# The opening of a hybrid decoder kernel, reordered: three row tiles in the first norm batch, a constant that loads ScalarE's table, parameters and decays behind the first products

## The chip, the cores and the metric

The kernel runs on one core of a Trainium2 chip. A core has engines that run side by side, each working off its own queue in order: TensorE (PE in the profile; its weight loads are PEld), VectorE (DVE), ScalarE (ACT), GpSimd (POOL), and SyncE (SP), which here issues nearly all DMAs. Products land in PSUM; VectorE and ScalarE can read it, and GpSimd's operands here lie in SBUF. The metric is the time of one execution on the device in microseconds.

## The reference, cut to what matters

One inference step of a decoder with one recurrent (RG-LRU) layer and one attention layer, for a prompt of 2048 tokens and 64 new tokens of 8 running sequences. Everything is f32 with a model width of 1024. Only the recurrent layer's beginning is touched:

```python
def rms_norm(x, g):
    xf = x.astype(jnp.float32)
    y = xf * lax.rsqrt(jnp.mean(xf * xf, axis=-1, keepdims=True) + EPS)
    return (y * g.astype(jnp.float32)).astype(x.dtype)

def recurrent_mixer(x, h0, conv_buf, w_in, conv_w, conv_b, w_ga, b_ga, w_gx, b_gx, lam, w_out):
    z = x @ w_in                                  # x is rms_norm(x, a_pre_norm)
    u, g = z[..., :D_RNN], z[..., D_RNN:]
    u, new_buf = causal_conv(u, conv_buf, conv_w, conv_b)
    h, h_last = rg_lru(u, h0, w_ga, b_ga, w_gx, b_gx, lam)
    return (h * jax.nn.silu(g)) @ w_out, h_last, new_buf
...
# in rg_lru, r and i are sigmoids of block products of u:
    log_a = -RGLRU_C * r * jax.nn.softplus(-lam.astype(jnp.float32))
    a = jnp.exp(log_a)
    inp = jnp.sqrt(-jnp.expm1(2.0 * log_a)) * (i * uf)
    # h is the running scan h <- a * h + inp
```

After the recurrent layer come the shared keys and values, attention of the prompt over itself, attention of the new tokens over a paged cache of 4096 rows per sequence, and the output projection.

## The kernel before, in words

The prompt is worked off in two halves of 1024 tokens. The first half takes the 64 new tokens along, so it has 1088 columns in three groups of 320, 384 and 384 columns. Its nine row tiles are the sample tile (64 rows) and eight prompt tiles of 128 rows; group 0 consists of the sample tile and two prompt tiles, groups 1 and 2 of three prompt tiles each.

`Norm0` (from L513) loads row tiles, four buffers deep (`A0_BUFS`), and normalises them in batches. ScalarE squares each tile's two halves with an accumulator (L544), VectorE adds the two sums, `rsqrt` (L222) computes the inverse root of the whole batch's column of sums by two starting operations and three Newton steps (L225 to L235), and VectorE scales each tile by the root and by the broadcast norm weight `apreB` (L552). `turned` then has TensorE transpose each tile by 128x128 blocks into PSUM (L508). ScalarE casts each block to the rounded type float32r (`xh`, L98), and VectorE writes the remainder (`xl`, L105). When a tile has been turned, its buffer's next load is issued. The first batch is made by the caller (`a00.norm(2)`), every later one by `turned`, two tiles each, so the batches hold 2, 2, 2, 2 and 1 tiles.

A product in f32 is made of three float32r products (`mm3`: high times high, high times remainder, remainder times high). Weights are split the same way: ScalarE casts a staged half of a weight (`wh`), and the remainder `wl` is written by VectorE and GpSimd in turns (`Weights.split`, L98 and L105).

`phase_a1` (L567) goes over the eight blocks of 128 recurrent channels, and in each over the three groups. For block n and a group it makes the product `u` (24 matmuls), copies it out, runs the short convolution on VectorE (`front`, L576 and L578, which reads the parameters `gv`), the gates of the group before (`gated`), the product `g`, and then the decay of the group before (`decayed`: two exponential-like activations on ScalarE that read `nsp4` and `psp4`, L614 and L615). A group's products start once `turned` has covered its columns.

`prologue` (L260) loads ten small parameters as 43 rows (L264 to L273), transposes them on TensorE in eight blocks (L276) into `gv`, and derives two halved biases. It is called through `ready` from `recur`, behind the fetch of the first weights and ahead of all products. `decays` (L282) turns the 8x128 lambdas into softplus values: one exponential on ScalarE and 25 operations on VectorE of 128x8 elements, the logarithm being a series (`log1p_into`, L240). It is traced in the first block right behind the front of group 0.

The order of the work on each engine is not written out by hand. The program is traced in the order of the code; a planner then times it with a model, and places what is ready by priority, which is the order of tracing, unless a `high_priority` block raises it. `issue_after(ins)` makes the instructions of its block on the engine of `ins` stand behind `ins`. What is placed is fixed: on the chip each engine goes through its queue in that order and waits where an operand is late.

Behind the opening follow `phase_a2` (the output product of the layer), the key, value and query projections together with the attention over the cache (`Side`, whose interleaving is set by estimated costs), the second half of the prompt, and the attention of the prompt.

Of the kernel before, what the change touches and what calls it, by code (L numbers as in the profile page):

```python
# [20 lines left out]
P = 128  # L21
D = 1024
# [5 lines left out]
H = 16  # L28
# [56 lines left out]
def tile_hawk_fox(  # L85
# [173 lines left out]

    def prologue():  # L260

        with tc.tile_pool(name="pro", bufs=1, side="right") as pro:
            rows = pro.tile([43, D], F32, name="rows")
            S.dma_start(rows[0:1, :], a_pre_norm)  # L264
            S.dma_start(rows[1:5, :], a_conv_w[0])
            S.dma_start(rows[5:6, :], a_conv_b)
            S.dma_start(rows[6:7, :], a_b_ga)
            S.dma_start(rows[7:8, :], a_b_gx)
            S.dma_start(rows[8:9, :], a_lambda)
            S.dma_start(rows[9:10, :], kv_norm.rearrange("(o d) -> o d", o=1))  # L270
            S.dma_start(rows[10:11, :], b_pre_norm)
            S.dma_start(rows[11:35, :], state_conv[0].rearrange("b j d -> (b j) d"))
            S.dma_start(rows[35:43, :], state_rnn[0])  # L273
            tp = mmp()
            for k in range(KB):
                T.transpose(tp[:, k * 43:(k + 1) * 43], rows[:, k * P:(k + 1) * P], ident[:43, :43])  # L276
# [3 lines left out]
            S.dma_start(bfB[:, :], b_f.rearrange("(o h) -> o h", o=1).broadcast_to([P, H]))  # L280

# [83 lines left out]
    def mm3(ps, lh, ll, rh, rl, nk):  # L365
        for k in range(nk):
            T.matmul(ps, lh(k), rh(k), start=(k == 0), stop=False)  # L367
            T.matmul(ps, lh(k), rl(k), start=False, stop=False)  # L368
            T.matmul(ps, ll(k), rh(k), start=False, stop=(k == nk - 1))  # L369
# [16 lines left out]
    class Weights:  # L386
# [125 lines left out]
    class Norm0:  # L512


        def __init__(self, s, pool):
            self.s, self.pool = s, pool
            self.apreB = pool.tile([P, D], F32, name="apreB")
            self.xts, self.n = [], 0
            self.load(0)
            S.dma_start(self.apreB[:, :], a_pre_norm.broadcast_to([P, D]))  # L520
            for i in range(1, A0_BUFS):
                self.load(i)
# [8 lines left out]
        def norm(self, n):  # L531
# [16 lines left out]
            tt(V, ss[:, :w], parts[:, 0, :w], parts[:, 1, :w], ALU.add)  # L548
            r = rsqrt(ss[:, :w], P, 1.0 / D, w=w)
            for k, i in enumerate(todo):  # L550
# [15 lines left out]

    def phase_a1(s, xs, a0, covered, feed, wk, out, then, begin):  # L567
        mh = s.mh
        sm = s.samp

        def front(n, c0, C, ups, us, up, W):
# [92 lines left out]
        for n in range(KB):  # L664
# [8 lines left out]
            for gi, (c0, C) in enumerate(s.groups):  # L673
# [1001 lines left out]

    def recur(s, a0, xs, covered, ex, out, then, begin, ready=None):

        with ExitStack() as ek:
            wk = sbuf(ek, f"a1_{s.i}")
            xs.extend(alloc_groups(sbuf(ex, f"xa_{s.i}"), s, len(xs), len(s.groups)))  # L1680
            feed = Feed([(a_in[n],) for n in range(KB)])
            feed.fetch()
            feed.fetch()
            if ready:
                ready()

            def turnover():
                ex.close()
                then()

            phase_a1(s, xs, a0, covered, feed, wk, out, turnover, begin)

# [26 lines left out]
    xs = []  # L1719
    recur(sca[0], a00.turned(xs, todo), xs, 0, ExitStack(), out, turn0, lambda: next(a2[0]), prologue)  # L1720
    x0.extend(alloc_x(sbuf(xe0, "xb0"), scb[0].cols))
# [119 lines left out]
```

## Time and profile before

| quantity | value |
|---|---|
| median of three runs | 3070.52 us (3066.45 to 3083.66) |
| the profiled execution | 3073.57 us |
| its span, first to last instruction | 3071.8 us |
| TensorE busy | 2826.8 us, 92% of the span |
| VectorE, ScalarE, GpSimd busy | 1805.2, 1294.9, 1158.7 us |
| mean granted TensorE clock | 0.965 |

A row of the timeline reads: start, duration, engine, line, operation, what it writes and reads, count; in brackets the idle time ahead of it and what ended that. Rows for short operations that follow each other on one engine can be merged, and their durations overlap. A row of groups has the busy time, the mean in ns, and the idle time ahead. A row of waits has the total, the number and the longest. A row of stages has the length, the busy time and count of PE, PEld, DVE, ACT and POOL, the granted clock, the share of the DMA engines' time and GB/s.

### The profile page before, as it was taken

How to read it: one execution, taken by the hardware profiler on the slowest of the kernel's cores; microseconds unless marked ns; L12 is line 12 of the kernel's file. 1: busy time of each engine (PE TensorE's matmuls, PEld its weight loads, DVE VectorE, ACT ScalarE, POOL GpSimd, SP SyncE). 2: the span in 40 equal slices, each digit the busy share in tenths (PEclk: the TensorE clock that was granted, in tenths of full speed). 3: DMA queues.
4: the chain of work that ended last, by engine and by line, in shares of the span. 5: the costliest groups of instructions: out<-in, count | busy, mean ns of one | idle time of the engine just before them, and what ended most of it. 6: DMA issues, size and time to landing. Idle time of an engine off the chain costs nothing.

```text
span 3071.8 us, 58144 instructions
## 1 busy us (share of the span) xinstructions
PE 2826.8 (92%) x20462; PEld 2178.9 (71%) x20462; DVE 1805.2 (59%) x4012; ACT 1294.9 (42%) x2874; POOL 1158.7 (38%) x1263
## 2 busy tenths in 40 slices
PE   5998999999999989997999798998989989999898
PEld 5997889988999978896888454555545554554587
DVE  7876555424357756755555566666667765543244
ACT  4665432222346655333333244343434445455321
POOL 1653201000025532000000365656565757788522
PEclk9999999999999999998999799999999999999999
DMA  4224547788622256999999998989999997322243
GB/s 121 91 76 147 157 137 209 239 256 260 209 82 86 86 180 202 318 312 313 329 311 316 303 285 258 293 276 306 294 309 316 328 286 236 107 67 68 83 143 111
DMA packets 492855, 653.25 MB, mean 213 GB/s; under 512 B 91100, under 2 KB 292829, under 8 KB 485286
## 3 DMA queue, kind: packets, MB, share of 16 engines
q1 hardware_dynamic: 488934, 643.87, 66.8%
q10 hardware_dynamic: 3340, 3.56, 0.4%
q8 instruction: 162, 2.65, 0.4%
q0 software_dynamic: 288, 2.10, 0.2%
q14 instruction: 131, 1.07, 0.1%
HBM read 513.82 MB, written 135.16 MB: 211 GB/s over the span
## 4 chain that ended last, share of the span: by engine, by line
PE 56%; DMA 18%; DVE 10%; ACT 6%; SPq 5%; issue 4%; POOL 2%; DVEq 0%; ACTq 0%; POOLq 0%
PE ops L1558 6%; DMA raw<-in_cache_k_dram 4%; PE y L367 4%; PE y L368 4%; PE y L369 4%; PE st L1538 4%; DMA raw<-in_cache_v_dram 4%; PE sx L1405 3%; PE kv L369 3%; PE kv L367 3%; PE kv L368 3%; PE dO L1236 3%; PE st L1539 3%; PE dS L1126 2%; PE qg L367 2%
## 5 line engine op out<-in xcount | busy, mean ns | idle before, releaser
L105 POOL TENSOR_TENSOR acc<-acc,p 128x512 f32<-128x512 f32 (+3 forms) x576 | 640.6, 1112 | 304.6 <-PE ops L1558 240.8
L1547 ACT ACTIVATE p<-st 128x512 f32<-128x512 f32 (+3 forms) x576 | 290.5, 525 | 409.5 <-PE st L1539 186.6
L1158 DVE STREAM_TRANSPOSE ktr<-raw 128x1024 f32<-128x1024 f32 x256 | 305.3, 1224 | 151.2 <-DMA raw<-in_cache_k_dram 141.8
L1407 DVE TENSOR_REDUCE mxs<-sx 128x1 f32<-128x512 f32 x384 | 253.6, 679 | 145.0 <-PE sx L1405 144.2
L368 PE MATMUL kv<-wl,xh 128*128 128x256 f32 (+3 forms) x1088 | 309.9, 288 | 9.0 <-DVE wl L412 8.8
L367 PE MATMUL kv<-wh,xh 128*128 128x256 f32 (+3 forms) x1088 | 311.0, 290 | 5.8 <-ACT wh L411 5.7
L369 PE MATMUL kv<-wh,xl 128*128 128x256 f32 (+3 forms) x1088 | 310.1, 287 | 0.0
L1558 PE MATMUL ops<-p,vvt 128*64 128x512 f32 (+3 forms) x1152 | 296.9, 554 | 2.3 <-ACT p L1547 2.1
L1538 PE MATMUL st<-qa,ka 128*128 128x512 f32 (+3 forms) x640 | 273.6, 428 | 21.1 <-ACT p L1547 16.6
L1405 PE MATMUL sx<-kbt,qbt 96*128 96x512 f32 (+3 forms) x640 | 232.3, 421 | 26.3 <-DMA qbt<-qd 10.6
L1538 PEld LDWEIGHTS st<-qa,ka 128*128 128x128 f32 x640 | 124.1, 194 | 179.5 <-issue 112.9
L411 ACT ACTIVATE wh<-wst,gv 128x256 fp32r<-128x256 f32 (+1 forms) x384 | 164.4, 499 | 187.7 <-DMA wst<-in_b_w_in_dram 73.2
L1539 PE MATMUL st<-qbt,kbt 128*128 128x512 f32 (+3 forms) x640 | 236.5, 371 | 0.0
L412 DVE SCALAR_TENSOR_TENSOR wl<-wst,gv,wh 128x256 fp32r<-128x256 f32 (+1 forms) x384 | 170.4, 494 | 104.6 <-ACT wh L411 100.8
L367 PE MATMUL qg<-xh,wh 128*128 128x384 f32 (+2 forms) x640 | 228.8, 359 | 0.0
L369 PE MATMUL qg<-xh,wl 128*128 128x384 f32 (+2 forms) x640 | 227.6, 357 | 1.1 <-DVE wl L412 1.0
L368 PE MATMUL qg<-xl,wh 128*128 128x512 f32 (+2 forms) x640 | 227.0, 356 | 0.0
L1091 POOL TENSOR_TENSOR qw<-qb,amask 128x128 f32<-128x128 f32 x64 | 29.8, 473 | 502.7 <-PE dS L1126 354.0
L368 PEld LDWEIGHTS kv<-wl,xh 128*128 128x128 f32 (+1 forms) x1088 | 204.3, 189 | 12.7 <-DVE wl L412 10.4
L367 PEld LDWEIGHTS kv<-wh,xh 128*128 128x128 f32 (+1 forms) x1088 | 204.3, 189 | 12.2 <-ACT wh L411 6.5
L369 PEld LDWEIGHTS kv<-wh,xl 128*128 128x128 f32 (+1 forms) x1088 | 206.0, 190 | 4.4 <-issue 4.3
L1405 PEld LDWEIGHTS sx<-kbt,qbt 96*128 96x128 f32 x640 | 117.6, 201 | 93.7 <-issue 31.1
(299 smaller groups left out, 6477.2 us busy)
## 6 DMA issues: line engine op xcount, KB each, us to landing
raw<-in_cache_k_dram SPq DMA_DIRECT2D x512, 256.0 KB
raw<-in_cache_v_dram SPq DMA_DIRECT2D x512, 256.0 KB
wst<-in_w_kv_dram SPq DMA_DIRECT2D x48, 512.0 KB
wst<-in_b_w_in_dram SPq DMA_DIRECT2D x48, 512.0 KB
xt<-in_x_prompt_dram SPq DMA_DIRECT2D x32, 512.0 KB
wst<-in_a_w_in_dram SPq DMA_DIRECT2D x64, 256.0 KB
out_dram<-kf SPq DMA_DIRECT2D x128, 128.0 KB
sc<-cd SPq DMA_DIRECT2D x16, 1024.0 KB
```

The costliest lines, as they stand in the source:

```text
L105: eng.tensor_tensor(out, a, b, op=op)
L367: T.matmul(ps, lh(k), rh(k), start=(k == 0), stop=False)
L368: T.matmul(ps, lh(k), rl(k), start=False, stop=False)
L369: T.matmul(ps, ll(k), rh(k), start=False, stop=(k == nk - 1))
L412: V.scalar_tensor_tensor(wl[:, k, :], st[:, k, :], gk, f(wh[:, k, :]), op0=ALU.mult, op1=ALU.subtract)
L1158: V.transpose(t.kts[pp][:, n], raw[:, :, pp * 256:(pp + 1) * 256])
L1405: T.matmul(ps[:, :w], qb[0:96, j * P:(j + 1) * P], kb[0:96, ck * 512:ck * 512 + w], start=True, stop=True)
L1407: V.reduce_max(mx[:, j, ck:ck + 1], ps[:, :w], axis=AX.X)
L1538: T.matmul(ps[:, lo:], ka[:, ks], qa[:, lo:], start=True, stop=False)
L1539: T.matmul(ps[:, lo:], kb[:, ks], qb[:, lo:], start=False, stop=(k < qc * 4))
L1547: pair.append((k, lo, p, A.activation(p[:, lo:], ps[:, lo:], AF.Exp)))
L1558: return T.matmul(ops[r:r + HD, lo:], vvs[h % 2][:, k, :], p[:, lo:], start=(k < 2), stop=(last and k >= todo[-1][0] - 1))
```

## The change

Five things are done, all in the opening of the first half:

- The first batch of `Norm0` has three tiles and so all of group 0; the nine tiles go in batches of 3, 2, 2 and 2. The load of `apreB` is issued behind three tile loads and not behind one.
- The inverse root in `Norm0.norm` is placed at high priority.
- ScalarE squares one column of a constant before anything else, so that its function table is loaded then.
- `prologue` is split. `parameters` issues the DMAs at the place where `prologue` issued them (and `bfB`'s with them, as before). The transposes and what hangs on them are traced behind the first `u` product. The pool that holds the rows stays open until then.
- `decays` is traced in group 1 behind the product `g`, ahead of the decay of group 0, and its VectorE operations stand behind the first operation of group 1's front.

```diff
-    def prologue():
-        with tc.tile_pool(name="pro", bufs=1, side="right") as pro:
-            rows = pro.tile([43, D], F32, name="rows")
-            S.dma_start(rows[0:1, :], a_pre_norm)
...
+    opening = ExitStack()
+
+    def parameters():
+        rows = opening.enter_context(tc.tile_pool(name="pro", bufs=1, side="right")).tile([43, D], F32, name="rows")
+        for lo, src in ((0, a_pre_norm), (1, a_conv_w[0]), (5, a_conv_b), (6, a_b_ga), (7, a_b_gx), (8, a_lambda),
...
+            S.dma_start(rows[lo:lo + src.shape[0], :], src)
+        S.dma_start(bfB[:, :], b_f.rearrange("(o h) -> o h", o=1).broadcast_to([P, H]))
+        return rows
+
+    def prologue(rows):
+        with opening:
             tp = mmp()
             for k in range(KB):
                 T.transpose(tp[:, k * 43:(k + 1) * 43], rows[:, k * P:(k + 1) * P], ident[:43, :43])
...
-            self.load(0)
-            S.dma_start(self.apreB[:, :], a_pre_norm.broadcast_to([P, D]))
-            for i in range(1, A0_BUFS):
+            for i in range(A0_BUFS):
+                if i == 3:
+                    S.dma_start(self.apreB[:, :], a_pre_norm.broadcast_to([P, D]))
                 self.load(i)
...
-            r = rsqrt(ss[:, :w], P, 1.0 / D, w=w)
+            with tc.high_priority():
+                r = rsqrt(ss[:, :w], P, 1.0 / D, w=w)
...
-            V.tensor_scalar(uc[:, so:C], up[:, 3:3 + tn], gv[:, n, 4:5], gv[:, n, 5:6], op0=ALU.mult, op1=ALU.add)
+            begun[0] = V.tensor_scalar(uc[:, so:C], up[:, 3:3 + tn], gv[:, n, 4:5], gv[:, n, 5:6],
+                                       op0=ALU.mult, op1=ALU.add).ins
...
                 mm3(ups[:, :C], W.h(0, P), W.l(0, P), rh, rl, KB)
+                if rows is not None:
+                    prologue(rows)
+                    rows = None
...
                 uc, uh, ul = front(n, c0, C, ups, us, up, W)
-                if so and n == 0:
-                    decays()
                 if pend:
                     trti = gated()
                 gps = mmp("g")
                 mm3(gps[:, :C], W.h(P, 2 * P), W.l(P, 2 * P), rh, rl, KB)
+                if pend and sm and n == 0 and gi == 1:
+                    with tc.issue_after(begun[0]):
+                        decays()
                 if pend:
                     decayed(*trti)
...
+    A.activation(small.tile([P, 1], F32, name="first", tag="first")[:, :], ones[:, 0:1], AF.Square)
     a00 = Norm0(sca[0], sbuf(es0, "a0_0", "right"))
-    todo = a00.norm(2)
+    todo = a00.norm(3)
```

More of the change, by code (lines that the diff above doesn't have):

```diff
@@ L258, in tile_hawk_fox @@
     psum["mm"] = banks(lin, "mm0", 6)
-    def prologue():
-        with tc.tile_pool(name="pro", bufs=1, side="right") as pro:
-            rows = pro.tile([43, D], F32, name="rows")
-            S.dma_start(rows[0:1, :], a_pre_norm)
[L265 to L273, printed above, removed]
+    opening = ExitStack()
+    def parameters():
+        rows = opening.enter_context(tc.tile_pool(name="pro", bufs=1, side="right")).tile([43, D], F32, name="rows")
+        for lo, src in ((0, a_pre_norm), (1, a_conv_w[0]), (5, a_conv_b), (6, a_b_ga), (7, a_b_gx), (8, a_lambda),
+                        (9, kv_norm.rearrange("(o d) -> o d", o=1)), (10, b_pre_norm),
+                        (11, state_conv[0].rearrange("b j d -> (b j) d")), (35, state_rnn[0])):
+            S.dma_start(rows[lo:lo + src.shape[0], :], src)
[3 more added lines that the diff above has]
+        with opening:
             tp = mmp()
@@ L279, in prologue @@
             V.tensor_scalar(hb_gx[:, :], gv[:, :, 7], 0.5, 0.0, op0=ALU.mult, op1=ALU.add)
-            S.dma_start(bfB[:, :], b_f.rearrange("(o h) -> o h", o=1).broadcast_to([P, H]))
     def decays():
@@ L565, in turned, with phase_a1 @@
                 yield done
-    def phase_a1(s, xs, a0, covered, feed, wk, out, then, begin):
+    def phase_a1(s, xs, a0, covered, feed, wk, out, then, begin, rows):
         mh = s.mh
         sm = s.samp
+        begun = [None]
         def front(n, c0, C, ups, us, up, W):
@@ L1674, in tile_hawk_fox, with recur @@
     b_in[0][0].append((256, w_kv[:, 2 * D:]))
-    def recur(s, a0, xs, covered, ex, out, then, begin, ready=None):
+    def recur(s, a0, xs, covered, ex, out, then, begin):
         with ExitStack() as ek:
@@ L1683, in recur @@
             feed.fetch()
-            if ready:
-                ready()
+            rows = parameters() if s.i == 0 else None
             def turnover():
@@ L1689, in turnover @@
                 then()
-            phase_a1(s, xs, a0, covered, feed, wk, out, turnover, begin)
+            phase_a1(s, xs, a0, covered, feed, wk, out, turnover, begin, rows)
     def shared(parts, nk, early=False):
@@ L1719, in tile_hawk_fox @@
     xs = []
-    recur(sca[0], a00.turned(xs, todo), xs, 0, ExitStack(), out, turn0, lambda: next(a2[0]), prologue)
+    recur(sca[0], a00.turned(xs, todo), xs, 0, ExitStack(), out, turn0, lambda: next(a2[0]))
     x0.extend(alloc_x(sbuf(xe0, "xb0"), scb[0].cols))
```

## The prediction

> **What bounds the kernel now.** I read the page first: the span, the busy shares and the chain of waits over the whole run.
>
> ```profile
> span 3071.8 us, 58144 instructions
> PE 2826.8 (92%) x20462; PEld 2178.9 (71%) x20462; DVE 1805.2 (59%) x4012; ACT 1294.9 (42%) x2874; POOL 1158.7 (38%) x1263
> PE 56%; DMA 18%; DVE 10%; ACT 6%; SPq 5%; issue 4%; POOL 2%; DVEq 0%; ACTq 0%; POOLq 0%
> ```
>
> TensorE is busy 92% of 3071.8 us, so in most stages nothing but its work sets the end. The change touches only the start, and a share over the whole run says nothing about that. So I went to the busy time by stage, with one stage ending where TensorE stops waiting.
>
> ```profile
> 10.00:62.00 52.00, 30.32 (x183) 26.88 (x184) 47.46 (x146) 27.49 (x62) 10.95 (x16) 1.00 0.46 131
> 62.00:90.00 28.00, 28.00 (x171) 28.00 (x170) 17.31 (x36) 16.36 (x27) 11.77 (x17) 1.00 0.16 44
> 90.00:260.00 170.00, 162.73 (x974) 160.82 (x973) 136.21 (x261) 106.22 (x182) 99.55 (x144) 1.00 0.25 81
> ```
>
> The columns after the length are busy time on PE, PEld, DVE, ACT, POOL, then clock, DMA share, GB/s. From 10 to 62 us VectorE is busy 47.46 of 52 us and TensorE only 30.32. From 62 to 90 TensorE is full, and to 260 it has 162.73 of 170. The opening is VectorE's stage; what follows is TensorE's, and it starts whenever the opening lets it. The chain of waits from 5 to 62 us and the waits of TensorE say what the opening hangs on.
>
> ```profile
> by line: DVE xt L552 15.8%; DVE xl L105 11.2%; SPq L399 10.7%; DMA wst<-in_a_w_in_dram 9.2%; DMA xt<-in_x_prompt_dram 7.7%; DVE uc L578 5.2%; DVE lp_s L105 4.0%; ACT junk L544 3.8%; ACT xh L98 3.8%; PE tps L508 3.3%; issue 2.5%; DVE sp_l L1
> ```
>
> ```profile
> PE tps L508 <- DVE xt L552: 23.7, 2, 15.2
> PE tps L508 <- DVE xl L105: 4.5, 5, 2.0
> ```
>
> The scaling of the x tiles (L552) leads the chain, and TensorE waits 23.7 us for it in two waits. The timeline shows the second of them: the tile that group 0 still lacks.
>
> ```profile
> 1.86 0.58 SPq L520 DMA_DIRECT2D apreB<-in_a_pre_norm_dram  x1
> 5.16 1.28 ACT L544 ACT_TABLE_LOAD   x1 [5.16 <-DMA xt<-in_x_sample_dram]
> 8.74 0.63 ACT L544 ACTIVATE junk<-xt 128x512 bf16<-128x512 f32 x1 [0.81 <-DMA xt<-in_x_prompt_dram]
> 10.32 0.16 DVE L105 TENSOR_TENSOR ss<-sq 128x2 f32<-128x2 f32 x1 [7.94 <-ACT junk L544]
> 13.26 0.16 DVE L105 TENSOR_TENSOR ss<-sq 128x2 f32<-128x2 f32 x1 [0.40 <-ACT junk L544]
> 13.78 2.47 DVE L552 SCALAR_TENSOR_TENSOR xt<-xt,nr_y,apreB 64x1024 f32<-64x1024 f32 x2
> 16.11 2.42 POOL L105 TENSOR_TENSOR wl<-wst,wh 128x1024 fp32r<-128x1024 f32 x1 [14.29 <-ACT wh L98]
> 16.24 3.37 DVE L105 TENSOR_TENSOR wl<-wst,wh 128x1024 fp32r<-128x1024 f32 x1
> 19.64 1.05 PE L276 MATMUL mm<-ident,rows 43*128 43x43 f32 x8 [3.35 <-DMA gst<-in_a_w_ga_dram]
> 19.95 1.21 DVE L105 TENSOR_TENSOR wl<-wst,wh 128x1024 fp32r<-128x1024 f32 x1
> 26.42 2.34 POOL L105 TENSOR_TENSOR wl<-wst,wh 128x1024 fp32r<-128x1024 f32 x1 [4.00 <-ACT wh L98]
> 26.44 2.34 DVE L105 TENSOR_TENSOR lp_s<-lp_s,sp_e 128x8 f32<-128x8 f32 x1
> 29.33 2.91 DVE L552 SCALAR_TENSOR_TENSOR xt<-xt,nr_y,apreB 128x1024 f32<-128x1024 f32 x2
> 31.19 1.94 PE L508 MATMUL tps<-ident,xt 128*128 128x128 f32 x8 [8.53 <-DVE xt L552]
> 34.57 0.39 PE L368 MATMUL u<-xl,wh 128*128 128x320 f32 x1
> 41.87 1.04 PE L508 MATMUL tps<-ident,xt 128*128 128x128 f32 x8
> 61.90 0.42 PE L367 MATMUL u<-xh,wh 128*128 128x384 f32 x1
> ```
>
> Group 0 (320 columns) needs the sample tile and two prompt tiles. The second batch's sums are ready at 13.26, but its tiles are scaled at 29.33: its short operations stand in turns with splits, evictions and the decays. Group 0's products run from 34.57; group 2's begin at 61.90, the last wait of this kind.
>
> **The change part by part.** Everything is counted in VectorE's stretch up to group 2's first product, since that is where the stage that TensorE fills begins.
>
> ```profile
> L105 DVE TENSOR_TENSOR xl<-tps,xh 128x512 fp32r<-128x512 f32 x15 | 10.3, 687 | 2.7 <-ACT xh L98 2.4
> L552 DVE SCALAR_TENSOR_TENSOR xt<-xt,nr_y,apreB 128x1024 f32<-128x1024 f32 x8 | 10.4, 1333 | 0.1
> L105 DVE TENSOR_TENSOR xl<-tps,xh 128x256 fp32r<-128x256 f32 x2 | 0.8, 406 | 0.0
> L251 DVE TENSOR_SCALAR sp_l<-sp_l 128x8 f32<-128x8 f32 x6 | 1.0, 168 | 0.0
> L229 DVE SCALAR_TENSOR_TENSOR nr_t<-nr_y,nr_m 128x1 f32<-128x1 f32 x3 | 0.7, 219 | 0.1
> L233 DVE TENSOR_SCALAR nr_t<-nr_t 128x1 f32<-128x1 f32 x3 | 0.5, 152 | 0.1
> ```
>
> Four rows of the timeline, for a lone chain and for the spacing of products:
>
> ```profile
> 51.28 0.15 DVE L233 TENSOR_SCALAR nr_t<-nr_t 128x1 f32<-128x1 f32 x1
> 52.73 0.16 DVE L105 TENSOR_TENSOR nr_y<-nr_y,nr_t 128x1 f32<-128x1 f32 x1
> ...
> 62.48 0.31 PE L368 MATMUL u<-xl,wh 128*128 128x320 f32 x1
> 62.63 0.31 PE L369 MATMUL u<-xh,wl 128*128 128x320 f32 x1
> ```
>
> (1) *Three tiles in the first batch.* Nine tiles go in 3+2+2+2, four batches, not five. A batch of one tile is 12 short operations; with three of 0.219 us and nine of about 0.152 it is 2.0 us. Minus 2.0; bounds 0 (it ran in VectorE's gaps) and minus 2.5: a lone chain goes seven steps from 51.28 to 52.73, 0.207 us each, 12 of them.
>
> (2) *Start of the first batch.* The apreB transfer (512 KB) goes behind two more tiles in SP's queue, the constant takes the table load off the path. The load itself (1.28 us) buys little: ScalarE then waits 0.81 us for a tile. What buys is the transfer: 512 KB is 1.4 us at the 369 GB/s of 5 to 10 us (row below), so the first prompt tile comes at about 7.3 us, the second is squared by 10.3, and the sum is as early as before with a tile more. Scaling starts then after 15 lone operations of 0.207, at 13.5, against 13.78: minus 0.3, bounds plus 1.0 and minus 1.3. apreB, now behind 2.8 us of other transfers, is wanted at 13.5 only.
>
> ```profile
> 5.00:10.00 5.00, 0.00 (x0) 0.00 (x0) 0.00 (x0) 3.96 (x8) 0.00 (x0) 1.00 1.00 369
> ```
>
> (3) *High priority for the root.* No work goes; but group 0 is complete early: three scalings of 1.28 to 17.3, W's split 1.21 to 3.37, two evictions of 0.406 and four of 0.687 (3.6 us): products from about 23.3, not 34.57. That is 11.3 us on TensorE's first product. It is not the gain: group 1 and 2 still need VectorE's other work.
>
> (4) *Parameters behind the first products.* The eleven DMAs keep their place in SP's queue, between the weights and the gate weights: nothing for the queue. The eight transposes (1.05 us, after 3.35 us of idle) leave the place where a scaled tile stood behind them. They now stand behind 24 products and ahead of group 0's front, which waits for them and the copy, some 1.5 us; the 24 products of g (0.15 us apart, 3.5 us) cover that on TensorE, the next batch on VectorE. If the cover is gone, plus 1.5. I take 0.
>
> (5) *Decays behind group 1's front.* 25 operations of about 0.168 us are 4.2 us of VectorE; none is removed. They ran ahead of group 0's front. They now run between group 1's front and ScalarE's first exponential for group 0. ScalarE takes its queue in order, so a late result holds that exponential, the copies behind it (the last tiles' evictions among them) and TensorE. As filler between the last tiles half may fall into gaps: minus 2.1; bounds plus 5.2 (25 in a lone chain, all waited for) and minus 4.2.
>
> (6) *Gaps and collisions.* VectorE's waits for ScalarE's evictions (2.4 us) shrink as tiles come in order and their loads are issued earlier: minus 1.5, bounds 0 and minus 2.4. The 8-column lp_s operation took 2.34 us, beginning and ending with POOL's split: 2.2 us lost. With the decays moved it can't meet that split; another may. I take half, minus 1.1; bounds 0 and minus 2.2. A rule speaks against this: the Trainium skill, "SBUF — State Buffer", in its part on the shared port pair, says that a VectorE operation with two SBUF inputs and a GpSimd operation reading SBUF exclude each other, and that the loser waits for the whole of the other. The pairs at 16.11/16.24 and 26.42/26.44 agree with it. By it any root or scaling operation meets the split in lp_s's place: this term is then 0 and the sum 5.9 instead of 7.0.
>
> Sum: 2.0 + 0.3 + 2.1 + 1.5 + 1.1 = 7.0 us off the opening, and the time behind it moves with it, as TensorE is full from there. One more row bears on the restart: eight transposes took 1.94 us after 8.53 us of idle and 1.04 us at 41.87. I price a colder start of one group at 0.9 us, inside the bounds. The Trainium skill, "TensorE: Matmul & The Clock Gate", Part 1, says that an idle window of 3.4 us halves the clock until as much busy time has passed; by that an extra gap between groups 0 and 1 would cost 1.7 us and the sum would be 5.3. The clock column reads 1.00 throughout; only the durations agree.
>
> The profiled execution took 3073.57 us: its span, and 1.8 us around it. It stands 3.05 us above the median 3070.52. Its own time would be 3066.6; against the median the forecast is 3063.5 us.
>
> **The rivals.**
>
> *All of the first product's advance is carried* (0.17): VectorE's order leaves fronts behind the tiles. 11.3 us off, 3059.2; with the 4.5 us of waits on evictions too, 15.8 us, 3054.7. Against it: VectorE's 47.46 busy us of 52, of which little goes.
>
> *Nothing arrives* (0.20): group 0 early, but group 2 at 61.90 as before, because VectorE has the same tiles, splits and decays to do: 3070.5; with decays waited for in full, 5.2 more, 3075.7. For it: the chain's line.
>
> *Slower* (0.09). The order of all queues is made by a planner that times the whole program, so a shifted opening can place later work otherwise. The place is the stage where DMA is full:
>
> ```profile
> 1350.00:1425.00 75.00, 75.00 (x659) 62.54 (x648) 41.74 (x75) 26.38 (x67) 1.75 (x5) 1.00 0.98 324
> 1425.00:1500.00 75.00, 58.83 (x472) 47.62 (x471) 39.86 (x93) 21.16 (x55) 0.00 (x0) 0.84 1.03 311
> 1650.00:1725.00 75.00, 58.73 (x423) 44.22 (x421) 42.13 (x95) 17.88 (x49) 16.06 (x25) 0.86 0.99 288
> ```
>
> TensorE has 75 us in one stretch and 58.8 in two others: one stall in such a stretch is 16.2 us. One more, with no gain, makes 3086.7; it decides from about 22 us, if the opening does give its 7.
>
> *Faster by the same road* (0.12): one stall fewer, 16.2 and 7.0 off: 3047.3.
>
> **How the numbers follow.** My forecast has 0.42, the rivals 0.17, 0.20, 0.09 and 0.12. The bound of 0.5% is 15.4 us, about what a measurement of this kernel can tell from no change (the three runs shown span 17). Faster: the 0.12, and 0.04 of the first rival at its far end: 0.16. Slower: 0.09. Same: 0.75. The range leaves out the slower rival and about half of the lucky one: from 3048, just above 3047.3, to 3076, the second rival with the decays in full. The forecast's own range is 3059 to 3068.
>
> **What would show it.** After: one table load ahead of the first x tile; 15 root operations in a row at about 10.3; three scalings one after another from 13.5; group 0's products from 23.3; the parameters' transposes behind 24 products; VectorE still over 85% busy until group 2, whose first product comes at about 55 and not 62. Then the stretch to 260 looks as before, 7 us earlier. Group 2 at 50 means the first rival; at 62 or later the second, and the culprit would be seen as ScalarE waiting for nsp ahead of an xh cast. The prediction is wrong if the opening moves by 7 and the end by something else: then stages after 260 us differ.

## The result and the profile after

The changed kernel takes 3099.28 us (median of 8 runs, 3096.83 to 3114.79); the kernel before, on the same chip, 3073.61 us (8 runs, 3066.45 to 3083.66). The ratio is 1.0091 with an interval of 1.0072 to 1.011: slower, outside the range given. The profiled execution of after took 3099.08 us with a span of 3097.4; that of before had a span of 3071.8, so the traces differ by 25.6 us.

The page of the kernel after, its span, its busy times and its chain of work:

```profile
span 3097.4 us, 58151 instructions
PE 2845.5 (92%) x20462; PEld 2189.8 (71%) x20462; DVE 1808.1 (58%) x4000; ACT 1293.8 (42%) x2875; POOL 1156.2 (37%) x1263
PE 49%; DMA 17%; DVE 6%; SPq 4%; ACT 4%; issue 3%; POOL 1%; ACTq 0%; DVEq 0%; POOLq 0%
```

TensorE issues the same 20462 products, and they take 18.7 us longer (2826.8 before). So by these records most of the loss is not idle time: the same work ran slower.

Where it went is read from landmarks: the start of the same product (the n-th of its kind) in both traces. Negative is earlier than in the kernel before, in us; the number in brackets is its time there.

```
                             after
first u product      (33.0)   -2.8
group 1, first u     (46.2)   +3.5
group 2, first u     (61.9)   +3.3
first y             (278.7)   +4.3
last qg            (1695.0)   -3.1
st, 241st          (2194.1)   -0.0
st, 361st          (2419.9)  +15.6
st, 481st          (2645.1)  +29.1
last y             (3061.5)  +25.6
```

Two losses, then. The opening gives 4.3 us away instead of gaining 7; some 7 us come back between 279 and 1695. (Of all the traces shown here, that of the kernel before takes longest over this stretch: the others take 2.0 to 13.6 us less, e2 below, with the same order there, among them. So part of this is the one execution, and its cause stays open.) And 26 to 32 us are lost far away, in the attention that runs beside the decode part, in code that the diff does not touch.

**The opening.** Busy time by stage in the kernel after (columns as in the prediction), and the two largest waits of TensorE up to 62 us:

```profile
10.00:62.00 52.00, 32.32 (x170) 29.34 (x170) 41.30 (x107) 22.19 (x50) 12.05 (x16) 0.93 0.46 135
62.00:90.00 28.00, 26.71 (x165) 26.00 (x164) 20.26 (x52) 18.43 (x32) 9.45 (x13) 1.00 0.15 44
```
```profile
PE tps L508 <- DVE xl L105: 15.3, 7, 4.8
PE tps L508 <- DVE xt L553: 14.4, 1, 14.4
```

VectorE is busy 41.30 of 52 us, 79%, where it was 47.46: the decays have left this stretch for the most part, and it now waits. TensorE's waits for it are 29.7 us instead of 28.2; the wait for the scaled tile became one for the evicted blocks. The timeline of the kernel after shows why:

```profile
0.81 1.28 ACT L1715 ACT_TABLE_LOAD   x1 [0.81 <-PEq L1829]
9.99 0.16 DVE L105 TENSOR_TENSOR ss<-sq 128x3 f32<-128x3 f32 x1 [7.62 <-ACT junk L544]
12.97 3.67 DVE L553 SCALAR_TENSOR_TENSOR xt<-xt,nr_y,apreB 64x1024 f32<-64x1024 f32 x3
17.67 0.36 ACT L98 CAST xh<-tps 128x256 fp32r<-128x256 f32 x1
19.08 0.33 SPq L528 DMA_DIRECT2D xt<-in_x_prompt_dram  x1
20.32 1.12 PE L508 MATMUL tps<-ident,xt 128*128 128x128 f32 x4 [4.84 <-DVE xl L105]
23.37 0.63 ACT L544 ACTIVATE junk<-xt 128x512 bf16<-128x512 f32 x1 [5.34 <-DMA xt<-in_x_prompt_dram]
24.75 0.56 ACT L98 CAST xh<-tps 128x512 fp32r<-128x512 f32 x1
24.88 0.16 DVE L105 TENSOR_TENSOR ss<-sq 128x2 f32<-128x2 f32 x1 [3.16 <-ACT junk L544]
26.34 2.37 POOL L105 TENSOR_TENSOR wl<-wst,wh 128x1024 fp32r<-128x1024 f32 x1 [3.87 <-ACT wh L98]
26.54 2.18 DVE L105 TENSOR_TENSOR nr_y<-nr_y,nr_t 128x2 f32<-128x2 f32 x1
30.15 0.61 PE L367 MATMUL u<-xh,wh 128*128 128x320 f32 x1
30.53 0.33 SPq L528 DMA_DIRECT2D xt<-in_x_prompt_dram  x1
30.70 1.08 PE L277 MATMUL mm<-ident,rows 43*128 43x43 f32 x8
32.14 0.47 PE L368 MATMUL u<-xl,wh 128*128 128x320 f32 x1
32.57 2.47 DVE L553 SCALAR_TENSOR_TENSOR xt<-xt,nr_y,apreB 128x1024 f32<-128x1024 f32 x2
36.66 0.31 PE L368 MATMUL g<-xl,wh 128*128 128x320 f32 x1
40.76 1.04 PE L508 MATMUL tps<-ident,xt 128*128 128x128 f32 x8
41.96 2.47 DVE L553 SCALAR_TENSOR_TENSOR xt<-xt,nr_y,apreB 128x1024 f32<-128x1024 f32 x2
45.09 0.66 PE L508 MATMUL tps<-ident,xt 128*128 128x128 f32 x4 [3.29 <-DVE xl L105]
49.69 0.69 PE L367 MATMUL u<-xh,wh 128*128 128x384 f32 x1
52.94 0.52 PE L367 MATMUL u<-xh,wh 128*128 128x384 f32 x1
53.67 0.34 PE L367 MATMUL u<-xh,wh 128*128 128x384 f32 x1
65.25 0.42 PE L367 MATMUL u<-xh,wh 128*128 128x384 f32 x1
69.26 0.65 ACT L617 ACTIVATE a<-tr,nsp 128x320 f32<-128x320 f32 x1 [3.14 <-DVE psp L293]
```

The first batch goes as forecast: the table load is at 0.81, three tiles are scaled from 12.97. Then ScalarE stops. With three tiles in the first batch the second is tiles 3 and 4, and tile 4 is the fifth tile of a pool of four buffers: its transfer is issued at 19.08, behind the first tile's turn and the transfers of the parameters and gates in SP's queue. ScalarE's queue has the squares of tile 4 ahead of the evictions of group 0's prompt tiles, and so it waits 5.34 us for that transfer. Tile 1's first blocks stand in PSUM from 21.4, the next cast is at 24.75, and VectorE is idle for 3.16 us until 24.88. Group 0's first product runs at 30.15, the parameters' transposes stand behind that one product of `u`, and but for one of `g` the rest follow from 32.14. The scaling of tiles 3 and 4 ends at 35.0, but their transposes stand behind all of group 0's products, at 40.76. Group 1's last tile, tile 5, is now scaled together with tile 6, whose load is issued at 30.53, when tile 2 has been turned and its buffer is free. The two are scaled at 41.96; the kernel before scales tiles 4 and 5 at 37.43:

```profile
37.43 2.48 DVE L552 SCALAR_TENSOR_TENSOR xt<-xt,nr_y,apreB 128x1024 f32<-128x1024 f32 x2
```

On VectorE this scaling stands ahead of the remainders of tile 3. TensorE waits 3.29 us for these, and group 1's first products (0.52 us each up to 53.3, then 0.34) go at half the clock; the row of the stage has 0.93, which is 2 x 0.07 x 52, about 7 us, at half rate. Group 0's products are slow at first, too: 0.47 us each from 32.14 to 36.1, then 0.31, as 36.66 shows. The first record of the clock in this trace begins at 36.3 us (34.5 in the kernel before), and the column reads 1.00 for the time ahead of it. The 15 slow products are 0.27 us apart instead of 0.15, which loses 1.8 us of the early start.

**The attention beside the decode part.** The stage from the last qg product to the 481st st product, first in the kernel before, then in the kernel after:

```profile
1694.97:2645.14 950.17, 861.84 (x7230) 490.23 (x7229) 629.42 (x1297) 415.19 (x994) 580.67 (x554) 0.94 0.90 282
```
```profile
1691.83:2674.21 982.38, 879.99 (x7233) 499.58 (x7232) 634.53 (x1305) 415.75 (x994) 581.31 (x554) 0.91 0.87 273
```

Nearly the same work (7230 and 7233 products fall in it), 32.2 us longer: the products are 18.2 us longer (861.84 to 879.99, at a granted clock of 0.91 instead of 0.94), and TensorE is idle 102.4 us instead of 88.3, 14.1 more. The waits of that stage (1700 to 2600 us; us in total, times, longest), before:

```profile
DVE ktr L1158 <- DMA raw<-in_cache_k_dram: 54.1, 30, 5.8
```
```profile
PE dO L1236 <- DMA raw<-in_cache_v_dram: 17.6, 14, 5.1
PE sx L1405 <- DVE mxs L1407: 5.4, 10, 1.3
```

and after:

```profile
DVE ktr L1165 <- DMA raw<-in_cache_k_dram: 70.3, 38, 4.2
```
```profile
PE dO L1243 <- DMA raw<-in_cache_v_dram: 28.8, 15, 3.9
PE sx L1412 <- DVE mxs L1414: 9.8, 15, 2.8
PE mps L1429 <- DVE mrow L1425: 9.7, 6, 3.1
```

VectorE's and TensorE's queues come to a cache tile before it has landed more often or by more: 16.2 us more on VectorE, 11.2 on TensorE. VectorE's queue also holds the maxima that TensorE waits for (`mxs`, `mrow`), and those waits grow too (`mrow` from 2.6 us). The issue orders of the two programs hardly differ behind the opening until about the middle of their instructions, and widely from there on.

### The profile page after: what moved, and what is told of

It is laid out like the page before. It is cut to its first block, busy times and chain, and to the rows that moved or that the text cites. A ratio compares the mean times of both kernels' runs of the same rounds, so it can differ in the third digit from the quotient of the medians.

```text
span 3097.4 us, 58151 instructions
## 1 busy us (share of the span) xinstructions
PE 2845.5 (92%) x20462; PEld 2189.8 (71%) x20462; DVE 1808.1 (58%) x4000; ACT 1293.8 (42%) x2875; POOL 1156.2 (37%) x1263
## 4 chain that ended last, share of the span: by engine, by line
PE 49%; DMA 17%; DVE 6%; SPq 4%; ACT 4%; issue 3%; POOL 1%; ACTq 0%; DVEq 0%; POOLq 0%
PE ops L1565 6%; DMA raw<-in_cache_k_dram 4%; PE st L1545 4%; DMA raw<-in_cache_v_dram 3%; PE sx L1412 3%; PE y L367 3%; PE y L368 3%; PE y L369 3%; PE st L1546 3%; PE dO L1243 3%; PE kv L367 2%; PE kv L369 2%; PE kv L368 2%; PE dS L1133 2%; SPq L1080 2%
## 5 line engine op out<-in xcount | busy, mean ns | idle before, releaser
L1412 PE MATMUL sx<-kbt,qbt 96*128 96x512 f32 (+3 forms) x640 | 240.1, 435 | 31.1 <-DVE mxs L1414 13.3
L367 PEld LDWEIGHTS kv<-wh,xh 128*128 128x128 f32 (+1 forms) x1088 | 204.0, 189 | 12.2 <-ACT wh L411 7.3
L368 PEld LDWEIGHTS kv<-wl,xh 128*128 128x128 f32 (+1 forms) x1088 | 203.9, 188 | 12.1 <-DVE wl L412 9.9
L1243 PE MATMUL dO<-raw,sx 128*32 128x256 f32 x2048 | 143.9, 403 | 54.7 <-DMA raw<-in_cache_v_dram 35.2
```

Of the source, the lines that this page charges most:

```text
L1243: return T.matmul(op[c:c + 32, :256], sx[:, d, i // 4, a * 4:(a + 1) * 4, :].rearrange("p h q -> p (h q)"), raw[:, d, a * 256:(a + 1) * 25 ...
L1412: T.matmul(ps[:, :w], qb[0:96, j * P:(j + 1) * P], kb[0:96, ck * 512:ck * 512 + w], start=True, stop=True)
```

## The experiments

My theory after the result: the opening itself costs about 4 us, and the rest is the planner's other order of the late work, which the opening's edit set off but does not need. The rival: the late stage is slower because of when it starts, or by the changed opening's transfers, whatever its order.

**The order of the late work held (e1, e2).** Everything traced behind the first half's recurrent blocks gets a given order on each of the five queues, by ordering edges without semaphores. e1 is the kernel after with the late order of the kernel before, e2 the kernel before with the late order of the kernel after.

```diff
     x0.extend(alloc_x(sbuf(xe0, "xb0"), scb[0].cols))
+    MARKED.append(len(tc.nc.cur_bb.bb.instructions))
...
+    for engine, order in json.loads(zlib.decompress(base64.b64decode(ORDER))).items():
...
+        for a, b in zip(row, row[1:]):
+            tc.add_manual_dep(b, a.name, mybir.DependencyInfo(mybir.DependencyClass.NoSync, mybir.DependencyReason.DATA),
+                              reason="pin")
```

> The changed opening, with the issue order of every engine behind the first half's recurrent blocks pinned to the order that the planner gave the kernel before (ordering edges alone, no waits). Theory (the loss is the planner's other order in the late stages): only the opening's own 4.4 us remain, 3073.6 + 4.4 = about 3078, ratio 1.001 to 1.002. Rival (the loss comes from the opening itself, by a shifted phase or a colder clock, whatever the order): about 3099, ratio 1.009. If half of each: 3088.

> The opening of before, with the late issue order pinned to that of the changed kernel. Theory: the whole loss but the opening's share appears, 3099 - 4.4 = about 3095, ratio 1.007. Rival: 3073, ratio 1.000.

Measured: e1 3077.18 us, ratio 1.0013 (0.9992 to 1.0034) against the kernel before; e2 3107.32 us, 1.0103 (1.0075 to 1.0132). The stage from the last qg product to the 481st st product, in e1 and in e2:

```profile
1693.24:2658.29 965.05, 862.61 (x7230) 490.67 (x7229) 626.12 (x1297) 415.54 (x994) 579.97 (x554) 0.94 0.90 277
```
```profile
1694.49:2680.43 985.94, 877.79 (x7233) 499.20 (x7232) 635.05 (x1305) 416.17 (x994) 580.16 (x554) 0.92 0.88 272
```

The loss goes with the order and not with the opening. With the order of after, the untouched opening loses what the changed one loses: 877.79 us for the products and 108.2 idle. With the order of before, the products take 862.61 us as in the kernel before. The waits for the cache go the same way: `ktr` on VectorE 58.8 us in e1 and 71.5 in e2, `dO` on TensorE 19.7 and 29.6. e1's idle time is 102.4 us all the same; this execution stands 5 us above e1's median.

**Which queue (e5, e6).** The kernel after, with the order of before in TensorE's queue alone (e5), and in SP's queue alone, the one that issues the transfers (e6). The edit is that of e1 with one engine in `ORDER`.

> The changed kernel, and of the late stages TensorE's order alone pinned to that of before; the planner orders the other queues around it. If TensorE's order is what decides (it sets which buffers come free when, and so what the other queues do): 3075 to 3082, as with all queues pinned. If the order of the DMA queue or of VectorE decides: 3090 to 3100. Half-rate clock between 1700 and 2600 us: about 110 us in the first case, 145 to 157 in the second.

> The changed kernel, and of the late stages only the order of SP's DMA issues pinned to that of before. If the DMA order decides: 3075 to 3082. If TensorE's order decides: stays above 3085, half-rate clock between 1700 and 2600 us above 125 us.

Measured: e5 3126.8 us, 1.0186 (1.0164 to 1.0208); e6 3094.2 us, 1.008 (1.006 to 1.01). e5's stage, and VectorE's largest wait for a transfer in it:

```profile
1693.03:2691.72 998.69, 874.37 (x7231) 489.09 (x7229) 628.28 (x1297) 415.56 (x994) 581.28 (x554) 0.92 0.86 268
```
```profile
DVE ktr L1190 <- DMA raw<-in_cache_k_dram: 90.5, 40, 10.4
```

With TensorE's order of before, and the other queues placed around it by the planner, the kernel is the slowest of all: 124.3 us idle, and VectorE waits 90.5 us for the cache. Neither branch had expected so much. e6 stays slow, as it should if the order of the transfers does not decide; but its clock was at half rate for only 113 us between 1700 and 2600 us, where over 125 was expected, in an execution 10 us below e6's median. So neither TensorE's queue nor SP's carries the loss alone. VectorE's, ScalarE's and GpSimd's were not held alone. My reading, which no run shows by itself, is that an order is good or bad as a whole, by the place that the five queues give to a transfer, to its use on VectorE and to what TensorE needs of it.

**Parts of the change (e3, e4, e7, e8).** e3 moves only the load of `apreB`, e4 only the parameters; both leave the planner free. e7 has the batch of three with the constant, the priority and the moved load; e8 moves only the decays; both with the late order held to that of before.

```diff
-            self.load(0)
-            S.dma_start(self.apreB[:, :], a_pre_norm.broadcast_to([P, D]))
-            for i in range(1, A0_BUFS):
+            for i in range(A0_BUFS):
+                if i == 3:
+                    S.dma_start(self.apreB[:, :], a_pre_norm.broadcast_to([P, D]))
                 self.load(i)
```
```diff
                 mm3(ups[:, :C], W.h(0, P), W.l(0, P), rh, rl, KB)
+                if rows is not None:
+                    prologue(rows)
+                    rows = None
```
```diff
-    todo = a00.norm(2)
+    todo = a00.norm(3)
```
```diff
-                if so and n == 0:
-                    decays()
...
+                if pend and sm and n == 0 and gi == 1:
+                    with tc.issue_after(begun[0]):
+                        decays()
```

> Before, and only the broadcast weight's load two places later in the queue; the planner's late order changes all the same. Theory: the first 300 us move by 1 us at most, and the end by anything between -15 and +30 us, all of it gained or lost between 1700 and 2600 us. Rival (the order does not matter): 3073 within 5 us.

> Before, and only the parameters' transposes moved behind the first u product; batches stay 2, 2, 2, 2, 1 and the decays stay in front of group 0's gates. In the first 300 us: 0 to 3 us off, as a scaled tile no longer stands behind the transposes. Theory: the end differs from that by the other late order, -15 to +30 us, between 1700 and 2600 us. Rival: the end moves with the opening, 3070 to 3073.

> Before, with the first batch of three tiles, apreB's load, the priority of the root and the constant; parameters and decays as before; late order pinned to before, so that the opening alone differs. Read at the first product of the layer's output stage, 278.7 us before and +3 to +4.3 in the two kernels with the whole change. If the batching costs the opening's loss (the turn of the next tiles stands behind all of group 0's products): +3 to +5 us there, and already +2 to +4 at group 1's first product (46.2 us before). If the decays or the parameters cost it: within 1 us at group 1.

> Before, with the decays alone moved to group 1; late order pinned to before. If the decays in their new place hold ScalarE: +2 to +5 us at 278.7 us. If they are covered and take load off VectorE before group 1: -1 to -3 us at group 1's first product and within 1 us at 278.7.

Measured: e3 3079.3 us, 1.0018 (0.9998 to 1.0038); e4 3096.66 us, 1.0095 (1.0062 to 1.0129); e7 and e8 in one run each 3081.1 and 3070.97 us. The landmarks against the kernel before, in us, are of one execution each. How far executions of the same opening lie apart can be read at the first y product: before and e2 at 0 and +1.5, after, e1, e5 and e6 at +4.3, +3.0, +4.2 and +2.8. At the end 8 executions of the kernel before spread over 17 us, so the totals of e7 and e8 say little.

```
                       e3     e4     e7     e8     e1    e12
group 1, first u     +0.4   -0.7   +2.1   -0.9   +2.3   -1.6
first y              -0.4   +1.4   +3.8   +2.0   +3.0   -1.6
last qg              -9.0  -12.2   -4.1   -3.2   -1.7  -10.7
st, 241st            -0.1  -12.5   +1.0   -2.5   +1.3  -11.2
st, 361st            +3.8   +8.3   +2.3   -2.6   +4.4   -9.7
st, 481st           +16.5  +16.6   +7.7   -1.9  +13.1   -1.4
last y              +12.4  +14.9   +7.6   -2.5   +8.7   -3.1
```

e3 and e4 have no loss in the opening to speak of, and lose 25.5 and 28.8 us between the last qg product and the 481st st product: each of these small edits, too, got another late order from the planner. Both had come 9.0 and 12.2 us early to the last qg product, which my theory (all of it between 1700 and 2600 us) had not. e4 is clearly slower; e3 is not (its interval reaches below 1, and the execution in the table is the slowest of its ten). In the opening the batch of three is what costs: with it (e7) group 1 is 2.1 us late, without it (e3, e4, e8) at most 0.4. e8 fits neither of its branches: 0.9 us early at group 1 and 2.0 late at the first y product, both near the spread.

**Two edits that should cure the opening (e9, e10, e11).** All three with the late order held. e9 gives the turn of the next tiles high priority, e10 has ScalarE issue the squares of the next batch behind the evictions of this one. e11 has both, without the move of the decays. (`cast[0]` is the last cast of an eviction.)

```diff
-                    turn(self.xts[i], m, *xs[g], col - self.s.groups[g][0])
+                    with tc.high_priority():
+                        turn(self.xts[i], m, *xs[g], col - self.s.groups[g][0])
```
```diff
-                todo = self.norm(2)
+                with tc.issue_after(cast[0].ins) if self.s.i == 0 else ExitStack():
+                    todo = self.norm(2)
```

> The kernel after, with every engine's late issue order held to that of the kernel before, and one edit in the opening: the turn (transposes) of the first half's next tiles has high priority, so that TensorE gets tile 3's eight transposes in the middle of group 0's products instead of behind all of them. Theory (the opening loses because tile 3's turn stands behind all of group 0's products, 40.76 us in the kernel after, and TensorE then starves until 49.69): group 1's first u product comes at 47 us or before, and the first y product 2 us or more earlier than with the kernel after's opening, at 281 us or before. Rival (what holds group 1 is the squares of tiles 3 and 4 in ScalarE's queue, waiting for tile 4's DMA, which stand ahead of the evictions either way): TensorE now waits for tile 3 inside group 0, and group 1 and the first y stay where they were, 49 to 50 us and 282 to 284 us.

> The kernel after, late issue order held to that of the kernel before, and one edit in the opening: ScalarE issues the squares of the next batch of tiles behind the evictions of this batch's, instead of ahead of them. Theory (ScalarE's queue is what holds group 0: in the kernel after the squares of tile 4 wait 5.34 us for its DMA and the eviction of group 0's tiles only comes at 24.75): group 0's first product comes 4 us or more earlier, at about 27 us, and group 1's and the first y product follow by 2 to 4 us, 46 to 47.5 us and 279 to 281 us. Rival (tile 3's turn, which stands behind all of group 0's products, sets group 1's start, and the squares coming later make the scaling of tile 3 later still): group 0 starts early, group 1 does not move or comes later than 49.7, and the first y product stays at 282 us or later.

> Both edits together (the next tiles' turn at high priority, the squares of the next batch behind this batch's evictions), late issue order held to that of the kernel before, and without the move of the decays: they stand in group 0 as in the kernel before. If the two queues (ScalarE's squares, TensorE's turn) are all that the opening loses, the first y product comes at 277 us or before, earlier than the kernel before's 278.7. If the batch of three itself costs more than it gives (three tiles scaled on VectorE before the first is turned, and VectorE without work behind them), it stays behind 278.7, at 280 to 284 us.

Measured, one run each: 3078.97, 3093.58 and 3092.92 us. The landmarks in the order e9, e10, e11: group 1 +2.6, +7.3, +7.3 us; first y +4.1, +15.2, +14.9; last y +5.4, +20.0, +19.4. The rivals hold. In e9 tile 3's blocks come in the middle of group 0's products and nothing is won: TensorE then waits 3.42 us, until 46.99, ahead of tile 5's blocks, as VectorE scales tiles 5 and 6 from 42.87. In e10 the wait of ScalarE only changes its cause, and TensorE waits for tile 5, which is now scaled at 50.36; three rows of e10's timeline:

```profile
25.35 1.04 ACT L123 CAST wh<-wst 128x1024 fp32r<-128x1024 f32 x1 [5.90 <-DMA wst<-in_a_w_in_dram]
28.42 0.61 PE L397 MATMUL u<-xh,wh 128*128 128x320 f32 x1
51.80 1.94 PE L538 MATMUL tps<-ident,xt 128*128 128x128 f32 x8 [7.93 <-DVE xt L583]
```

The squares gone, the cast of the fourth weight block stands in their place and waits 5.90 us for its own transfer; the first product comes 1.7 us earlier than in the kernel after and not 4. So both my explanations of the opening's loss by one queue's place fell: in e9 and e10 TensorE still waits for tile 5. With more than four buffers this wasn't tried.

These runs show one thing more: with the order held, a later opening is carried to the end (e10: 15.2 at the first y, 12.1 at the last qg, 20.0 at the last y; e11 much the same).

**The rest of the change without the batch of three (e12).** As e1, with two tiles in the first batch:

```diff
-    todo = a00.norm(3)
+    todo = a00.norm(2)
```

> The kernel after with every engine's late issue order held to that of the kernel before, as in e1, and one edit: the first norm batch has two tiles again. If the batch of three is what the opening loses (with it alone group 1's first product came 2.1 us and the first y product 3.8 us later), the first y product comes at 277 to 280.5 us, against 281.7 in e1, and the time is 3 to 8 us under e1's, 3068 to 3074 us: level with the kernel before. If the other parts together lose the opening's time (the parameters' and decays' instructions, put between the products and the turns of the next tiles), the first y product stays at 281 to 283 us and the time at 3075 to 3080 us.

Measured: 3073.57 us, ratio 1.0002 (0.9985 to 1.0018): level with the kernel before. The opening and the late stage of e12, and two rows of its timeline:

```profile
10.00:62.00 52.00, 34.16 (x193) 30.34 (x194) 44.26 (x129) 25.11 (x54) 10.89 (x16) 1.00 0.46 132
```
```profile
1684.23:2643.77 959.54, 863.86 (x7230) 491.28 (x7229) 627.66 (x1295) 414.55 (x994) 579.07 (x554) 0.94 0.90 279
```
```profile
22.87 0.63 ACT L569 ACTIVATE junk<-xt 128x512 bf16<-128x512 f32 x1 [4.69 <-DMA xt<-in_x_prompt_dram]
34.05 2.48 DVE L578 SCALAR_TENSOR_TENSOR xt<-xt,nr_y,apreB 128x1024 f32<-128x1024 f32 x2
```

The first y product is 1.6 us early where e1's was 3.0 late, so this one line is 4.6 us of the opening; the clock there reads 1.00 again. ScalarE waits for tile 4 here too, 4.69 us, so that wait by itself is not what the third tile costs. What differs is tile 5: with two tiles in the first batch it is scaled with tile 4, at 34.05 instead of 40.80 in e1. It is so in every trace: in the eight kernels with three tiles tile 5 is scaled at 40.3 us or later and group 1's first product comes at 48.1 or later, in the six with two at 37.4 or before and at 46.6 or before. No run moved tile 5 alone.

The last qg product is 10.7 us early, and 9.3 of these are gone after the attention beside the decode part. That a head start is not kept there does not follow: e10 came to the stage 12.1 us late and took 958.1 us over it, e12 took 959.5, and the 950.2 of the kernel before is the shortest of all these executions. No version found here is clearly faster than the kernel before.

## Why the prediction was wrong

*What bounds the opening.* VectorE by its busy time: right for the kernel before, and the base of the error. The sum took work off VectorE and let the rest close up, as if VectorE were never made to wait. After the change it waits 3.16 us for ScalarE at 24.88, and its queue scales the last tile of group 1 late.

*(1) Three tiles.* Minus 2.0, bounds 0 and minus 2.5. Wrong in sign: with the other parts in place the batch costs 4.6 us at the first y product (e1 against e12), 3.8 with its three companions alone (e7). The step counted the short operations saved, and not which tiles the later batches then pair: tile 5, without which group 1 can't start, goes with tile 6, whose buffer comes free only when tile 2 has been turned (30.53), and is scaled at 41.96 instead of 37.43.

*(2) Start of the first batch.* Right: scaling from 12.97 against 13.5 forecast, one table load at 0.81, the sum at 9.99 and 14 root operations behind it, 15 in all, up to 12.97. The moved load by itself is worth nothing that these runs can tell (e3: first y product 0.4 us earlier); the constant was not tried alone.

*(3) High priority for the root.* "Products from about 23.3": they came from 30.15, and but for two from 32.14. The failed step: only VectorE's operations were added up, and ScalarE's casts, which VectorE's remainders wait for, were taken as always done. Up to 30.15 the trace has, beyond the sum, VectorE's 3.16 us of waiting for ScalarE, a second split of 1.21 us, and the root operations of the second batch, which their priority puts between the evictions, one of them 2 us longer by the collision below. The parameters' transposes take 1.4 us from 30.70 on. ScalarE's wait of 5.34 us is not all loss: without the squares there (e10) the first product came 1.7 us earlier.

*(4) Parameters.* The forecast of 0 with a bound of 1.5 holds (e4: 1.4 us later at the first y product, 0.7 earlier at group 1). That is within the spread. But they stand behind one product of `u` and not 24, so TensorE has no cover there.

*(5) Decays.* Minus 2.1, bounds minus 4.2 and plus 5.2: e8 has plus 2.0 at the first y product, inside, and near the spread. The feared wait is there: in the kernel after ScalarE waits 3.14 us for `psp` at 69.26.

*(6) Gaps and collisions.* VectorE's waits for evictions did not shrink (2.5 us where they were 2.4), and the wait of 3.16 us came on top. Half the collision was to go; in its place a root operation of 0.16 us takes 2.18, beside GpSimd's split at 26.34. The Trainium skill, "SBUF — State Buffer", on the shared port pair, had said so (the loser waits for the whole of the other), and this trace agrees: its 0 was the better value for that term. The restart was priced at 0.9 us; group 1's products run at half rate from 49.69 to 53.3, which loses half of 3.6 us, 1.8. The Trainium skill, "TensorE: Matmul & The Clock Gate", Part 1, says that one idle window halves the clock; the 0.52 us products behind a wait of 3.29 us agree with it, though the wait is a little under 3.4 us, and the 1.7 us that went with the rule was the better price. The 1.8 us that group 0's early products lose were in no term. The prediction took the clock column's 1.00 as a reading; ahead of 34.5 us it has no record behind it.

*"The time behind it moves with it, as TensorE is full from there."* This step failed by most. It holds, roughly, only with the order held (e10: 15.2 becomes 20.0). In the kernel after the order behind 1700 us is another, and that is 32.2 us, against 4.3 of the opening; with the order of before the ratio is 1.0013 (e1), and the order of after alone makes 1.0103 (e2).

*The rivals.* The one that ended slower was the true one, by its mechanism: a shifted opening makes the planner place later work otherwise. It was held for unlikely at 0.09, though the text itself said that the planner times the whole program. Its place was wrong (not the projections under full DMA, but the attention beside the decode part, with a DMA share of 0.87 to 0.90), and so was its price: not a stall of 16.2 us, but 14.1 us of idle in small pieces and 18.2 us of slower products. The same mechanism on the lucky side had got 0.12. The six late orders measured lean the other way: the stage takes 950 us in the kernel before, 951 to 965 where its order is held (e1, e7 to e12), and 966 to 999 in the five other orders (after with e2, e3, e4, e5, e6), one execution each. Only three of these five were drawn by the planner freely and one (e3) is not clearly slower over its runs, so that the order of before is a good one is likely, not shown.

*"Nothing arrives"* had group 2 at 61.90 as before; it came at 65.25. The culprit named there, the decays' result ahead of a cast, was not it: group 1 was late by 3.5 us already at 49.69, ahead of that wait at 69.26.

What stays open: why the lower clock comes with the other order. After and e1 have the same 102.4 us of idle time in the stage, at granted clocks of 0.91 and 0.94, so it isn't the amount of idle time alone; where it sits may decide, but the clock was not changed by itself in any run.

## What to carry to other kernels

Where a planner orders the whole program, an edit at one end is an edit everywhere: compare landmarks of both traces first, and hold the order of the rest to learn what the edit itself does. Before tiles are put into a larger first batch, write down which tiles each later batch then pairs and when the last of them can be loaded, and follow every queue in order, the casts as well as the engine that looks busiest. A wait for a transfer at the head of an in-order queue need not be cured by moving the instruction: here the next one waited for its own transfer.

## What the runs showed of the hardware

The clock halves without a long wait. Stretches of the kernel after, around 2371 us, and all that TensorE waited for from 2362 to 2371:

```profile
2364.20:2371.00 6.80, 5.82 (x24) 3.09 (x23) 4.18 (x14) 5.07 (x18) 4.83 (x7) 1.00 1.10 202
2371.00:2381.20 10.20, 7.66 (x34) 3.00 (x34) 5.29 (x15) 4.60 (x14) 0.00 (x0) 0.50 0.95 317
```
```profile
PE st L1545 <- ACT p L1554: 0.8, 2, 0.4
PE sx L1412 <- DVE mxs L1414: 0.4, 1, 0.4
```

TensorE is busy 5.82 of 6.80 us by the records, its longest wait is 0.4 us (one of 0.74 begins as the clock falls), and still it then runs 10.2 us at 0.50. By the clock records of the late stage 17 of 22 half-rate stretches in the kernel after (12 of 17 before) begin with no wait of 3.3 us or more that reaches into the 6.8 us ahead, and they last 3.4 us or a multiple of it, up to 34. The rule cited above names a whole idle window; here lesser gaps went ahead of it as well. What they must add up to, no run shows.
